# Values of two key blocks at a time, and a unit's tail behind the next unit's scores, in a two-layer hybrid attention kernel

## The chip, the cores and the metric

The kernel runs on one core of one Trainium2 chip. The metric is the device time of one execution in microseconds (us). Engines: PE is TensorE (matmuls; PEld are its weight loads), DVE is VectorE, ACT is ScalarE, POOL is GpSimd, SP is SyncE, which issues DMAs here.

## What is computed

Two layers of a hybrid block over 256 context tokens and 1024 latent tokens, 1024 wide, in fp32 (large projections are split in two parts of a shorter format, and three products of the parts are added). Each layer: a modulated RMSNorm, one input projection whose columns feed four head groups (A: latent attention with 4 heads; B: global grouped-query attention with 4 heads; C: windowed grouped-query attention with sinks, 4 heads; D: a bidirectional state-space scan), an output projection, a gated residual. The change touches the softmax attention of A, B and C:

```
def attention(q, k, v, scale):              # one head
    s = einsum('qd,kd->qk', q, k) * scale   # group C: a window, and the context
    p = softmax(s)                          # group C: a sink logit joins the sum
    return einsum('qk,kd->qd', p, v)
# context tokens read only context tokens; latent tokens read both
# y = attention(...) * silu(gate)
```

## The kernel before

The order of each engine's instructions is static. A scheduler sets it from the order of the code, the tiles' dependences and the number of buffers of each pool. Tokens lie in three groups: group 0 the 256 context tokens, groups 1 and 2 the 512 latent tokens each. The attention goes over six pairs of heads (B, A, C, two pairs each), and for each over the groups 1, 2 and 0 (in layer 1, where the context is no longer needed, 1 and 2). One call of `main` for a pair and a group is called a **unit** here: 18 in layer 0 and 12 in layer 1. Its keys come in blocks of 128: ten in A and B, seven in C, two for group 0.

For each block and each of two heads, `scores` makes transposed scores (128 keys by up to 512 queries) in a bank of PSUM named `ps_st` (L1215 to L1217 in A, L1220 to L1223 in B and C) and ScalarE writes their exponentials to a tile `P` (L1224). `values` multiplies the probabilities with the values (L1231): one matmul for each head, 64 columns of the array each, into the two halves of the accumulator `ps_acc`. Each of these fp32 matmuls is two records in the trace. Then `values` adds the probabilities of the block to a running sum `ac` (L1237, L1243), on GpSimd or VectorE. A block's values are issued after the next block's scores.

Behind the last block: group C adds the sink's exponential (`es`, L1265) to the running sums on VectorE (L1267); ScalarE copies the accumulator to `o` (L1269), GpSimd multiplies the gate (L1270). Three steps are the unit's **tail**, and the next unit issues them after its blocks 1, 2 and 4 (`TAIL_AT`): the token sums of head 0, those of head 1 (each transposes of `ac` into `ps_sum` on TensorE, L1277, then sums with an accumulating activation on ScalarE, L1280; at the end a reciprocal, L1283), and `finish` (a transpose of the reciprocals, L1287, a way through DRAM to spread them, L1295, and the product with `o`, L1297).

Between the blocks stand pieces of other work: for the next units, maxima of scores (matmuls L1143, reduced by VectorE, L1147, and transposed, L1171), and in the last pair of a layer the loads of the output projection's weights and their split in two halves (L1495; VectorE's L1502 and L1503).

[...] The accumulator's bank also serves transposes of the first stage and the scan's outputs. `P` tiles and raw weights come from a ring of large buffers, `bg`, with five.

Of the kernel before, what the change touches and what calls it, by code (L numbers as in the profile page):

```python
# [12 lines left out]
ALU = mybir.AluOpType  # L13
# [11 lines left out]
LEAD = 2  # L25
RD = 2
RD2 = 0
TAIL_AT = (1, 2, 4)
N_LATE = 3
AFTER = 3  # L30
X_AT = 0
# [26 lines left out]
def hybrid_block(ctx, tc, x, ctxt, c_t, w_fm, w_tm, w_mod, b_gate, p_col, p_row, w_qu, w_kvu, w_out,  # L58
                 fnw, consts, rope_tm, rope_fm, out, dbg=None):
    nc = tc.nc  # L60
# [47 lines left out]
    def free_all(slots):  # L108
        for s in slots:
            s.free()  # L110
# [4 lines left out]
    def ring(tag, bufs, cols):  # L115
        def f(shape=(P, cols), dt=F32, name=tag):
            return tp.tile(list(shape), dt, tag=tag, bufs=bufs, name=name)
        return f

    tm, ac, bg = ring("tm", 8, 512), ring("ac", 3, 1024), ring("bg", 5, 1024)  # L120

    PS_BUFS = {"MX": 3, "S2": 3, "ACC": 1, "TR": 2}

    def ps(tag, name=None):
        return pp.tile([P, 512], F32, tag=tag, bufs=PS_BUFS[tag], name=name or f"ps_{tag}")

# [909 lines left out]
    def attention(L, res, need_ctx, y, late):  # L1036
# [160 lines left out]
        def main(op, gi, pieces, tail):  # L1197
            lo, n = GROUPS[gi]
            nt = n // P
            br, kd = op["br"], op["kd"]  # L1200
            acc = ps("ACC", name="ps_acc")
            sums = [None]
            blocks = key_blocks(br, gi)

            def scores(bi):
                kb, c0, w, mo = blocks[bi]
                k = lambda tok, rows: tok.tile(kb, 0, rows)
                pts = bg((P, 2, 512), name="P")
                for h in range(2):
                    st = ps("S2", name="ps_st")[:, :w]  # L1210
                    q0, q1 = op["q"][h]
                    q = lambda tok, rows: tok(lo + c0, w, 0, rows)
                    if br == 0:
                        k0, k1 = op["k"][h]
                        mm(st, lhsT=k(k0, 96), rhs=q(q0, 96), start=True, stop=False)  # L1215
                        mm(st, lhsT=k(k1, 96), rhs=q(q0, 96), start=False, stop=False)  # L1216
                        mm(st, lhsT=k(k0, 97), rhs=q(q1, 97), start=False, stop=True)  # L1217
                    else:
                        k0, k1 = op["k"][0]
                        mm(st, lhsT=k(k0, 128), rhs=q(q0, 128), start=True, stop=False)  # L1220
                        if mo is not None:
                            mm(st, lhsT=ident_r, rhs=mask_r[:, mo:mo + w], start=False, stop=False)
                        mm(st, lhsT=k(k1, 65), rhs=q(q1, 65), start=False, stop=True)  # L1223
                    nc.scalar.activation(out=pts[:, h, :w], in_=st, func=AF.Exp, scale=op["scale"])  # L1224
                return pts

            def values(bi, pts):
                kb, c0, w, mo = blocks[bi]
                for h in range(2):
                    v0 = h * 64 if br == 0 else op["pair"] * 64  # L1230
                    mm(acc[h * 64:h * 64 + 64, c0:c0 + w], lhsT=op["v"].tile(kb)[:, v0:v0 + 64], rhs=pts[:, h, :w],  # L1231
                       start=(bi == 0), stop=(bi == len(blocks) - 1))
                if bi == 0:
                    sums[0] = pts
                elif bi == 1:
                    s = ac((P, 2, 512), name="ac")
                    nc.gpsimd.tensor_tensor(out=s[:, :, :n], in0=sums[0][:, :, :n], in1=pts[:, :, :n], op=ALU.add)  # L1237
                    sums[0] = s
                else:
                    s = sums[0]  # L1240
                    for h in range(2):
                        eng = nc.vector if h == 0 and bi % 2 == 0 else nc.gpsimd
                        eng.tensor_tensor(out=s[:, h, c0:c0 + w], in0=s[:, h, c0:c0 + w], in1=pts[:, h, :w], op=ALU.add)  # L1243

            prev = None
            total, done = len(pieces), 0
            for bi in range(len(blocks)):
                cur = scores(bi)
                if prev is not None:
                    values(bi - 1, prev)  # L1250
                prev = cur
                if bi in TAIL_AT and tail:
                    tail.pop(0)()
                want = min(total, -(-total * (bi + 1) // max(1, len(blocks) - LEAD)))
                while done < want:
                    pieces[done]()
                    done += 1
            for f in tail:
                f()
            values(len(blocks) - 1, prev)  # L1260
            if br == 2:
                for h in range(2):
                    hd = op["pair"] * 2 + h
                    es = tm(name="es")
                    nc.scalar.activation(out=es[64:65, :n], in_=f32(op["q"][h][1](lo, n, 64, 65)), func=AF.Exp,  # L1265
                                         scale=HEAD_SCALE, bias=pr[64:65, PR_SINK + hd:PR_SINK + hd + 1])
                    nc.vector.tensor_tensor(out=sums[0][64:65, h, :n], in0=sums[0][64:65, h, :n], in1=es[64:65, :n], op=ALU.add)  # L1267
            o = tm(name="o")
            nc.scalar.copy(o[:, :n], acc[:, :n])  # L1269
            nc.gpsimd.tensor_tensor(out=o[:, :n], in0=o[:, :n], in1=op["gate"](lo, n), op=ALU.mult)  # L1270

            ss = small([P, 8], "asum", "asum", 2)

            def token_sums(h):
                pss = ps("TR", name="ps_sum")
                for t in range(nt):
                    nc.tensor.transpose(pss[:, t * P:(t + 1) * P], sums[0][:, h, t * P:(t + 1) * P], ident)  # L1277
                for t in range(nt):
                    junk = tm((P, P), name="junk")
                    nc.scalar.activation(out=junk, in_=pss[:, t * P:(t + 1) * P], func=AF.Copy, scale=2.0,  # L1280
                                         accum_out=ss[:, h * nt + t:h * nt + t + 1])
                if h == 1:
                    nc.vector.reciprocal(out=ss[:, :2 * nt], in_=ss[:, :2 * nt])  # L1283

            def finish():
                pr_ = ps("TR", name="ps_rt")
                nc.tensor.transpose(pr_[0:2 * nt, 0:P], ss[:, :2 * nt], ident)  # L1287
                row = tm((8, P), name="rrow")
                nc.scalar.copy(row[0:2 * nt, :], pr_[0:2 * nt, 0:P])
                dr = d_rs[n_unit[0] % 4]  # L1290
                n_unit[0] += 1
                nc.sync.dma_start(out=dr[0:2 * nt, :], in_=row[0:2 * nt, :])
                rb = tm(name="rb")
                for h in range(2):
                    nc.sync.dma_start(out=rb[h * 64:h * 64 + 64, :n],  # L1295
                                      in_=dr[h * nt:(h + 1) * nt, :].rearrange("t q -> (t q)").unsqueeze(0).to_broadcast([64, n]))
                nc.vector.tensor_tensor(out=y[br * 2 + op["pair"]](lo, n), in0=rb[:, :n], in1=o[:, :n], op=ALU.mult)  # L1297
            return [lambda: token_sums(0), lambda: token_sums(1), finish]

        sink8 = const([P, 4])  # L1300
        nc.vector.tensor_scalar(out=sink8, in0=pr[:, PR_SINK:PR_SINK + 4], scalar1=8.0, scalar2=None, op0=ALU.mult)
        gorder = [1, 2, 0] if need_ctx else [1, 2]
# [9 lines left out]
        y_slots, tail = [], []  # L1312
        for i, (br, pair) in enumerate(pairs):
            op = ops[br, pair]
            if need_ctx and i == 0:
                pk = Slot([P, 4, NCTX], F32, "y_cx")
                y_slots.append(pk)
            if need_ctx and br == 2:
                pk = res["ssd"].y_slots[0]
            s = Slot([P, NLAT], F32, f"y{br}{pair}")  # L1320
            y_slots.append(s)
            y[br * 2 + pair] = Tok(pk.t[:, br * 2 + pair - (2 if br == 2 else 0), :] if need_ctx else None, s.t)
            for gi in gorder:
                pieces = []
                if gi == 1:
                    for g in gorder[1:]:
                        pieces += maxima(op, g)
                elif gi == 2 and i + 1 < len(pairs):
                    pieces = prep(*pairs[i + 1])
                if i + 1 == len(pairs):  # L1330
                    pieces = pieces + sum((late() for _ in range(N_LATE)), [])
                tail = main(op, gi, pieces, tail)
            free_all(op["free"])
        yield y_slots, tail


# [127 lines left out]
    for L in range(DEPTH):  # L1464
# [48 lines left out]
        y_slots, tail = next(gen[0])  # L1513
# [86 lines left out]
```

## Time and profile before

| what | us |
|---|---|
| median of three runs | 1862.44 |
| lowest and highest | 1859.09, 1864.99 |
| profiled execution | 1860.59 |
| its span | 1858.8 |
| mean granted clock of TensorE | 0.983 of full speed |

The span runs from the first to the last instruction that the trace has. The profile gives the busy time of each engine, tables of busy time in stretches of the span, groups of instructions by line, and a timeline. In the timeline a row is one or several instructions of the same line and shape that follow each other: start, length, engine, line, what it writes and reads, count; in square brackets is the idle time of the engine ahead of it and what ended that. PE rows end by a model, so the steps between starts are the better measure.

### The profile page before, as it was taken

The page shows a single profiled execution, that of the slowest core. Times are in us where ns is not written, and L with a number is a line of the kernel's source. Part 1 is how long each engine was busy: PE and PEld are TensorE (multiplying, and loading weights), DVE is VectorE, ACT ScalarE, POOL GpSimd, SP SyncE. Part 2 cuts the span into 40 slices and gives each one's busy share as a digit, 9 for nine tenths or more (in the row PEclk, how much of TensorE's full clock was granted, in tenths as well). Part 3 has the DMA queues.
Part 4 walks back from the last instruction along what each step waited for, and adds up shares of the span by engine and source line. Part 5 has one row for each costly group of instructions (what it writes and reads, how often), then busy time and mean ns, then how long its engine had stood idle before and what let it go on. Part 6 is the DMA issues. An engine that isn't in the chain of part 4 may idle for free. (4 is left out here: it accounts for less than half of the span.)

```text
span 1858.8 us, 27849 instructions
## 1 busy us (share of the span) xinstructions
PE 1775.0 (95%) x9658; PEld 1326.4 (71%) x9658; DVE 1135.9 (61%) x2290; ACT 750.1 (40%) x2060; POOL 777.4 (42%) x735
## 2 busy tenths in 40 slices
PE   6999999999999999998999989999999999999898
PEld 4667888899974555565787778888998455556586
DVE  6867864374366655458547678754645666444854
ACT  5433433332224545456423333343332444445531
POOL 2313552042327666555223125521332576665522
PEclk9999999999999999998999999999999999999899
DMA  8464323265584232223411434231768533220521
GB/s 303 134 228 145 123 99 109 76 203 181 186 226 116 81 104 63 67 67 127 146 57 40 147 107 145 92 114 69 242 201 229 141 83 86 63 57 12 168 88 57
DMA packets 130396, 231.52 MB, mean 125 GB/s; under 512 B 13784, under 2 KB 74560, under 8 KB 130256
## 3 DMA queue, kind: packets, MB, share of 16 engines
q1 hardware_dynamic: 130256, 229.75, 39.9%
q8 instruction: 76, 1.25, 0.3%
q14 instruction: 64, 0.52, 0.1%
HBM read 161.15 MB, written 68.44 MB: 124 GB/s over the span
## 5 line engine op out<-in xcount | busy, mean ns | idle before, releaser
L1243 POOL TENSOR_TENSOR ac<-ac,P 128x512 f32<-128x512 f32 (+3 forms) x248 | 304.2, 1239 | 174.7 <-ACT P L1224 144.4
L1147 DVE TENSOR_REDUCE mp<-ps_s 128x1 f32<-128x512 f32 (+3 forms) x428 | 261.7, 658 | 187.1 <-PE ps_s L1143 167.1
L1224 ACT ACTIVATE P<-ps_st 128x512 f32<-128x512 f32 (+3 forms) x456 | 238.9, 553 | 221.6 <-PE ps_st L1223 90.4
L128 PE MATMUL ps_fm<-hh,wfm_hi 128*128 128x512 f32 x576 | 235.5, 409 | 2.8 <-DVE kb L658 2.1
L130 PE MATMUL ps_fm<-hl,wfm_hi 128*128 128x512 f32 x576 | 232.4, 403 | 2.6 <-POOL hl L403 2.4
L129 PE MATMUL ps_fm<-hh,wfm_lo 128*128 128x512 f32 x576 | 231.4, 402 | 0.0
L128 PE MATMUL ps_tm<-wtm_hi,hh 128*128 128x256 f32 x512 | 146.5, 286 | 0.7 <-DVE qkhl L783 0.7
L129 PE MATMUL ps_tm<-wtm_hi,hl 128*128 128x256 f32 x512 | 145.5, 284 | 0.0
L130 PE MATMUL ps_tm<-wtm_lo,hh 128*128 128x256 f32 x512 | 145.2, 284 | 0.0
L130 PEld LDWEIGHTS ps_fm<-hl,wfm_hi 128*128 128x128 f32 x576 | 110.2, 191 | 28.7 <-POOL hl L403 5.3
L128 PEld LDWEIGHTS ps_fm<-hh,wfm_hi 128*128 128x128 f32 x576 | 110.5, 192 | 26.5 <-ACT hf L399 3.2
L129 PEld LDWEIGHTS ps_fm<-hh,wfm_lo 128*128 128x128 f32 x576 | 110.2, 191 | 19.6 <-issue 0.8
L1237 POOL TENSOR_TENSOR ac<-P 128x1024 f32<-128x1024 f32 (+1 forms) x30 | 66.6, 2221 | 118.7 <-ACT P L1224 114.0
L128 PE MATMUL ps_o<-wo_hi,yh 128*128 128x512 f32 x288 | 113.9, 396 | 0.4 <-ACT yh L1354 0.4
L129 PE MATMUL ps_o<-wo_hi,yl 128*128 128x512 f32 x288 | 113.5, 394 | 0.1
L130 PE MATMUL ps_o<-wo_lo,yh 128*128 128x512 f32 x288 | 113.1, 393 | 0.0
L1231 PE MATMUL ps_acc<-P,vt 128*64 128x512 f32 (+3 forms) x416 | 101.2, 540 | 0.5 <-ACT P L1224 0.5
L128 PEld LDWEIGHTS ps_tm<-wtm_hi,hh 128*128 128x128 f32 x512 | 98.1, 192 | 2.8 <-DVE qkhl L783 1.1
L130 PEld LDWEIGHTS ps_tm<-wtm_lo,hh 128*128 128x128 f32 x512 | 98.2, 192 | 0.8 <-issue 0.4
L129 PEld LDWEIGHTS ps_tm<-wtm_hi,hl 128*128 128x128 f32 x512 | 98.2, 192 | 0.4
L1381 POOL TENSOR_TENSOR xres<-xres,dl 128x512 f32<-128x512 f32 x32 | 41.3, 1290 | 113.1 <-DVE dl L1380 113.1
L1243 DVE TENSOR_TENSOR ac<-ac,P 128x512 f32<-128x512 f32 (+3 forms) x88 | 60.5, 687 | 30.8 <-ACT P L1224 20.8
(345 smaller groups left out, 4174.9 us busy)
## 6 DMA issues: line engine op xcount, KB each, us to landing
wfm_raw<-in_w_fm_dram SPq DMA_DIRECT2D x36, 512.0 KB
wm<-in_w_mod_dram SPq DMA_DIRECT2D x64, 256.0 KB
d_q<-qkhl SPq DMA_DIRECT2D x18, 512.0 KB
wm<-in_w_mod_dram SPq DMA_DIRECT2D x16, 512.0 KB
d_gate<-th SPq DMA_DIRECT2D x32, 256.0 KB
wtm_raw<-in_w_tm_dram SPq DMA_DIRECT2D x16, 512.0 KB
qq<-d_q SPq DMA_DIRECT2D x32, 256.0 KB
wo_raw<-in_w_out_dram SPq DMA_DIRECT2D x16, 512.0 KB
```

Of the source, the lines that this page charges most:

```text
L128: mm(o, lhsT=lh, rhs=rh, start=first, stop=False)
L129: mm(o, lhsT=ll, rhs=rh, start=False, stop=False)
L130: return mm(o, lhsT=lh, rhs=rl, start=False, stop=last)
L1147: nc.vector.tensor_reduce(out=dst, in_=p[:, :nu * w].rearrange("p (u k) -> p u k", u=nu), axis=AX.X, op=ALU.max)
L1224: nc.scalar.activation(out=pts[:, h, :w], in_=st, func=AF.Exp, scale=op["scale"])
L1231: mm(acc[h * 64:h * 64 + 64, c0:c0 + w], lhsT=op["v"].tile(kb)[:, v0:v0 + 64], rhs=pts[:, h, :w], start=(bi == 0), stop=(bi == len(blocks) ...
L1237: nc.gpsimd.tensor_tensor(out=s[:, :, :n], in0=sums[0][:, :, :n], in1=pts[:, :, :n], op=ALU.add)
L1243: eng.tensor_tensor(out=s[:, h, c0:c0 + w], in0=s[:, h, c0:c0 + w], in1=pts[:, h, :w], op=ALU.add)
L1381: (nc.vector if t == ts[-1] else nc.gpsimd).tensor_tensor(out=xt.t[:, js], in0=xt.t[:, js], in1=d, op=ALU.add)
```

## The change

The values are issued in batches of two blocks (`BATCH`), a batch behind the scores of the following batch. The running sums leave `values` for `add`, which stands right behind a block's scores. The unit's last batch, the copy of the accumulator and the gate become a step `output` of the tail, which then has up to four steps: `output`, the token sums of both heads together, `finish`, and older ones that are left. At the end of a batch one step of the tail is issued, two if over three are left. A pair's keys are released in the `output` of its last unit. At the end of the layer's attention the tail is issued down to two steps. A second bank is allowed to the accumulator, and a sixth buffer to the ring `bg`.

```
-TAIL_AT = (1, 2, 4)
+BATCH = 2
...
-    tm, ac, bg = ring("tm", 8, 512), ring("ac", 3, 1024), ring("bg", 5, 1024)
-
-    PS_BUFS = {"MX": 3, "S2": 3, "ACC": 1, "TR": 2}
+    tm, ac, bg = ring("tm", 8, 512), ring("ac", 3, 1024), ring("bg", 6, 1024)
+
+    PS_BUFS = {"MX": 3, "S2": 3, "ACC": 2, "TR": 2}
...
+            def add(bi, pts):
+                kb, c0, w, mo = blocks[bi]
                 if bi == 0:
                     sums[0] = pts
...
-            prev = None
+            todo = []
+
+            def flush_values():
+                for bi, pts in todo:
+                    values(bi, pts)
+                todo.clear()
+
             total, done = len(pieces), 0
+            batch = []
             for bi in range(len(blocks)):
-                cur = scores(bi)
-                if prev is not None:
-                    values(bi - 1, prev)
-                prev = cur
-                if bi in TAIL_AT and tail:
-                    tail.pop(0)()
+                pts = scores(bi)
+                batch.append((bi, pts))
+                add(bi, pts)
+                if len(batch) == BATCH or bi == len(blocks) - 1:
+                    for _ in range(2 if len(tail) > 3 else 1):
+                        if tail:
+                            tail.pop(0)()
+                    flush_values()
+                    todo.extend(batch)
+                    batch = []
...
-            for f in tail:
-                f()
-            values(len(blocks) - 1, prev)
...
-            nc.scalar.copy(o[:, :n], acc[:, :n])
-            nc.gpsimd.tensor_tensor(out=o[:, :n], in0=o[:, :n], in1=op["gate"](lo, n), op=ALU.mult)
+            last_unit = gi == gorder[-1]
+
+            def output():
+                flush_values()
+                nc.scalar.copy(o[:, :n], acc[:, :n])
+                nc.gpsimd.tensor_tensor(out=o[:, :n], in0=o[:, :n], in1=op["gate"](lo, n), op=ALU.mult)
+                if last_unit:
+                    free_all(op["free"])
...
-            return [lambda: token_sums(0), lambda: token_sums(1), finish]
+            return tail + [output, lambda: [token_sums(h) for h in range(2)], finish]
...
-            free_all(op["free"])
+        while len(tail) > 2:
+            tail.pop(0)()
```

Lines behind the edit have other numbers: L1243 becomes L1246, L1267 L1278, L1277 L1295, L1280 L1298, L1287 L1305, L1502 and L1503 L1521 and L1522. The number of instructions of each kind is the same on each engine.

How the order moves, at three places. First TensorE in the body of layer 0, at a transpose of maxima (L1171, operand `mt`); here a row stands for one instruction or several, `ps_st` are scores, `ps_s` maxima, `ps_acc` values, where x2 is one block with its two heads. Before:

```order
L1231 MATMUL ps_acc<-P,vt 64x512
L1171 MATMUL ps_m<-con,mt 8x128
L1231 MATMUL ps_acc<-P,vt 64x512
L1143 MATMUL ps_s<-kk_cx 128x256 x4
L1220 MATMUL ps_st<-qq_5595,kk 128x512
L1223 MATMUL ps_st<-ql_5597,k_5594 128x512
L1220 MATMUL ps_st<-qq_5596,kk 128x512
L1223 MATMUL ps_st<-ql_5598,k_5594 128x512
L1231 MATMUL ps_acc<-P,vt 64x512 x2
L1220 MATMUL ps_st<-qq_5595,kk 128x512
L1171 MATMUL ps_m<-con,mt 4x128
```

After:

```order
L1143 MATMUL ps_s<-kk_cx 128x256 x4
L1220 MATMUL ps_st<-qq_5595,kk 128x512
L1223 MATMUL ps_st<-ql_5597,k_5594 128x512
L1220 MATMUL ps_st<-qq_5596,kk 128x512
L1223 MATMUL ps_st<-ql_5598,k_5594 128x512
L1220 MATMUL ps_st<-qq_5595,kk 128x512
L1223 MATMUL ps_st<-ql_5597,k_5594 128x512
L1220 MATMUL ps_st<-qq_5596,kk 128x512
L1223 MATMUL ps_st<-ql_5598,k_5594 128x512
L1231 MATMUL ps_acc<-P,vt 64x512
L1171 MATMUL ps_m<-con,mt 4x128
L1231 MATMUL ps_acc<-P,vt 64x512 x3
```

The values of two blocks now stand behind the scores of two; the second transpose, which stood between scores, now stands between two heads of a block.

Second, TensorE at the end of the attention of layer 0, in the last pair of group C, around the token sums (`ps_sum`). Before:

```order
L1220 MATMUL ps_st<-qq_8522,kk 128x256
L1222 MATMUL ps_st<-mask_r 128x256
L1223 MATMUL ps_st<-ql_8524,k_8521 128x256
L1277 MATMUL ps_sum<-con,ac 128x128 x4
L1231 MATMUL ps_acc<-P,pk_7967 64x512 x4
L1277 MATMUL ps_sum<-con,ac 128x128 x4
```

After:

```order
L1231 MATMUL ps_acc<-P,pk_7961 64x512 x4
L1220 MATMUL ps_st<-qq_8518,kk 128x384
L1222 MATMUL ps_st<-mask_r 128x384
L1223 MATMUL ps_st<-ql_8520,k_8517 128x384
L1295 MATMUL ps_sum<-con,ac 128x128 x4
L1220 MATMUL ps_st<-qq_8519,kk 128x384
L1295 MATMUL ps_sum<-con,ac 128x128 x4
```

The new unit's first values and the scores of a further block now stand ahead of the sums.

Third, VectorE ahead of the sink's addition for those sums. Before:

```order
L1503 TENSOR_TENSOR wo_lo<-wo_raw,wo_hi 128x512 x2
L1502 CAST wo_hi<-wo_raw 128x512 x2
L1503 TENSOR_TENSOR wo_lo<-wo_raw,wo_hi 128x512 x2
L1243 TENSOR_TENSOR ac<-ac,P 128x384
L1243 TENSOR_TENSOR ac<-ac,P 128x128
L1267 TENSOR_TENSOR ac<-ac,es 1x512 x2
```

After:

```order
L1301 RECIPROCAL asum<-asum 128x4
L1246 TENSOR_TENSOR ac<-ac,P 128x128
L1522 TENSOR_TENSOR wo_lo<-wo_raw,wo_hi 128x512
L1246 TENSOR_TENSOR ac<-ac,P 128x128
L1521 CAST wo_hi<-wo_raw 128x512 x2
L1522 TENSOR_TENSOR wo_lo<-wo_raw,wo_hi 128x512 x2
L1278 TENSOR_TENSOR ac<-ac,es 1x512 x2
```

The running sums stand earlier, and two halves of the output weights are now cast and subtracted between them and the sink's addition.

## Rows read from the trace of the kernel before

**Rows 1.** The page's first part: busy time, share of the span, instructions.

```profile
PE 1775.0 (95%) x9658; PEld 1326.4 (71%) x9658; DVE 1135.9 (61%) x2290; ACT 750.1 (40%) x2060; POOL 777.4 (42%) x735
```

**Rows 2.** Table by stretches: us, then busy of PE, PEld, DVE, ACT, POOL, clock, DMA.

```profile
700.00:750.00 50.00, 50.00 (x226) 28.67 (x225) 29.20 (x48) 25.20 (x78) 29.64 (x21) 1.00 0.31 73
...
850.00:875.00 25.00, 21.48 (x111) 12.40 (x109) 22.62 (x40) 13.19 (x43) 14.31 (x14) 0.86 0.32 101
...
1725.00:1750.00 25.00, 20.20 (x108) 12.81 (x108) 23.36 (x36) 12.00 (x42) 15.07 (x12) 0.86 0.39 127
```

**Rows 3.** Groups by line and shape: busy us, mean ns, idle before and releasers.

```profile
L1243 POOL TENSOR_TENSOR ac<-ac,P 128x512 f32<-128x512 f32 x192 | 253.4, 1333 | 130.2 <-ACT P L1224 115.1 <-DVE mp L1147 7.8 <-DVE ac L1243 4.9
L1224 ACT ACTIVATE P<-ps_st 128x512 f32<-128x512 f32 x352 | 200.0, 598 | 189.6 <-PE ps_st L1217 81.8 <-PE ps_st L1223 66.4 <-POOL ac L1243 13.6
...
L1503 DVE TENSOR_TENSOR wo_lo<-wo_raw,wo_hi 128x512 fp32r<-128x512 f32 x26 | 25.7, 1019 | 0.0
...
L1502 DVE CAST wo_hi<-wo_raw 128x512 fp32r<-128x512 f32 x26 | 14.7, 600 | 0.1
```

**Rows 4.** Timeline of PE, values of one block alone and of two together.

```profile
560.02 0.40 PE L1220 MATMUL ps_st<-qq,kk 128*128 128x512 f32 x1
560.25 0.40 PE L1223 MATMUL ps_st<-ql,k 65*128 65x512 f32 x1
560.58 1.08 PE L1231 MATMUL ps_acc<-P,vt 128*64 128x512 f32 x4
561.59 0.96 PE L1143 MATMUL ps_s<-kk,qq 128*128 128x512 f32 x3
...
574.90 1.94 PE L1231 MATMUL ps_acc<-P,vt 128*64 128x512 f32 x8
576.77 0.50 PE L1220 MATMUL ps_st<-qq,kk_cx 128*128 128x512 f32 x1
577.10 0.40 PE L1223 MATMUL ps_st<-ql,kk_cx 65*128 65x512 f32 x1
```

**Rows 5.** Timeline of PE, a pair of heads with another matmul between.

```profile
568.83 1.07 PE L1231 MATMUL ps_acc<-P,vt 128*64 128x512 f32 x2
569.84 0.27 PE L1171 MATMUL ps_m<-con,mt 128*8 128x128 f32 x1
570.04 1.07 PE L1231 MATMUL ps_acc<-P,vt 128*64 128x512 f32 x2
571.04 0.75 PE L1143 MATMUL ps_s<-kk_cx 128*128 128x256 f32 x4
```

**Rows 6.** Timeline of all engines, token sums at the end of layer 0's attention.

```profile
861.92 3.87 DVE L1267 TENSOR_TENSOR ac<-ac,es 1x512 f32<-1x512 f32 x2 [0.84 <-ACT es L1265]
...
864.26 1.09 PE L1277 MATMUL ps_sum<-con,ac 128*128 128x128 f32 x4 [3.33 <-DVE ac L1267]
...
865.27 3.68 PE L1231 MATMUL ps_acc<-P,pk 128*64 128x512 f32 x8
865.38 0.28 ACT L1280 ACTIVATE junk<-ps_sum 128x128 f32<-128x128 f32 x1 [1.93 <-PE ps_sum L1277]
...
866.43 0.21 ACT L1280 ACTIVATION_READ_ACCUMULATOR junk<-ps_sum 128x1 f32 x1
...
867.36 0.38 ACT L1224 ACTIVATE P<-ps_st 128x256 f32<-128x256 f32 x1 [0.71 <-PE ps_acc L1231]
```

**Rows 7.** Timeline of PE, the other three waits for the sink's addition.

```profile
879.57 1.30 PE L1277 MATMUL ps_sum<-con,ac 128*128 128x128 f32 x5 [2.29 <-DVE ac L1267]
...
1743.74 1.12 PE L1277 MATMUL ps_sum<-con,ac 128*128 128x128 f32 x4 [4.80 <-DVE ac L1267]
...
1759.60 1.69 PE L1277 MATMUL ps_sum<-con,ac 128*128 128x128 f32 x8 [3.19 <-DVE ac L1267]
```

**Rows 8.** Table by stretches of 5 us behind the two longest waits; columns as rows 2.

```profile
865.00:870.00 5.00, 5.00 (x19) 1.75 (x19) 4.97 (x10) 1.99 (x12) 1.87 (x3) 0.59 0.00 0
...
1745.00:1750.00 5.00, 5.00 (x17) 2.02 (x17) 3.62 (x9) 1.98 (x13) 1.71 (x1) 0.53 0.15 25
```

## The prediction

> **What bounds the kernel now.** I read the busy shares first. TensorE is busy 95% of the span, and no other engine is above 61% [rows 1]. The table by stretches says where: in the body of the attention TensorE is busy all of each 50 us at a granted clock of 1.00, while VectorE, ScalarE and GpSimd have slack [rows 2]. So there the time is what TensorE issues, and a change gains only by making the same matmuls closer or cheaper. The two exceptions are the ends of the two layers' attention (850 to 875 and 1725 to 1750): VectorE is busy 22.6 and 23.4 of 25 us there, TensorE only 21.5 and 20.2, and the clock falls to 0.86 [rows 2].
>
> The profiled execution took 1860.6 us, 1.8 under the median of the runs shown (1862.4), well inside what a measurement can tell from no change, about 0.3% or 5.6 us. The sum below is made against 1860.6.
>
> **What a group of value matmuls costs.** The change makes the same matmuls as before, so it counts only how they stand. In the scores, matmuls of 512 columns follow each other every 0.23 us (560.02 to 560.25). One block with both heads (x4, since each of its matmuls is two records) standing alone: the step into it is 0.33 instead of 0.23, and it takes 1.01 until the next matmul starts (560.58 to 561.59). Two blocks together (x8) take 1.87 (574.90 to 576.77), and the matmul behind the group also takes 0.33 instead of 0.23 [rows 4]. So a second block behind a first costs 0.86, a group by itself 0.86 + 0.15 + 0.10 + 0.10: **each separate group costs about 0.35 us beyond its blocks**. The two heads of a block run at once, on two halves of the array's columns: four records take what two do. Where another matmul stands between the heads that is lost: x2, 1.01 us; the other one, 0.20; x2, 1.00; 2.21 in all [rows 5]. Against 1.01 + 0.20 together **a cut pair costs 1.00 more**, 0.35 of it for being two groups.
>
> **The change part by part.**
>
> *Batches of two.* In the order of TensorE the value matmuls stand in 209 separate groups before and 140 after: 153 groups of one block and 29 of two become mostly batches of two blocks. 69 fewer groups at 0.35 are -24.2 us. But the scheduler also cuts pairs: a maximum's transpose (L1171), a reciprocal's (L1305) or one score is put between the heads in about 25 places after, in 13 before. 12 more at 1.00 - 0.35 (the other part is in the count of groups) are +7.8. Together -16. The blocks of the small group and of the window are narrower than those I priced, and the transposes and maxima now stand at other borders, whose steps I don't know: 40 of them dearer by the 0.10 of such a step would be +4, 90 of them +9. I take **-12**, with -16 and -7 for the ends.
>
> [...]
>
> *The tail of a unit behind the next unit's scores.* In the body nothing waits at units' borders, so the move is worth nothing there: the cover is TensorE's own work. It counts at the ends. Before, the token sums' transposes of the last windowed pair wait for the sink's addition (L1267): in layer 0 VectorE's two run from 861.92 for 3.87, and TensorE idles 3.33 at 864.26, 2.29 at 879.57, 4.80 at 1743.74 and 3.19 at 1759.60 [rows 6, 7], 13.6 us in all. After, the transposes stand later. I priced the matmuls between a unit's last scores and its first transpose, at 0.23 per 512 columns and groups as above: 3.9 us becomes 7.9 (layer 0, group 1), 2.3 becomes 4.2 (layer 0, group 2), 3.9 becomes 6.4 and 1.4 becomes 2.1 (layer 1). With the additions as late as now the waits would be 0, 0.4, 2.3 and 2.5, that is 5.2: a gain of 8.4. Against this VectorE has two more pairs of weight halves (L1502, L1503) ahead of the addition in layer 0, and each half pair costs it over a microsecond and a half (0.60 and 1.02 a piece) [rows 3]; that may take back 2 to 3. I take **-6**, ends -10 and 0.
>
> *The clock.* After the two long waits the clock is 0.59 and 0.53 for 5 us [rows 8], and the following x8 group takes 3.68 us instead of 1.94 [rows 4, 6], 1.7 lost each time. If one of the two places no longer waits long, that is **-2**, ends -4 and 0.
>
> *Sums of both heads at once, reciprocal close behind.* Eight sums of ScalarE come in one go: four take from 865.38 to 866.64, 1.26 us [rows 6], so eight take 2.5. The transpose of the reciprocals (L1305) needs the last of them, VectorE's reciprocal and a queue; in nine units of 30 the order leaves under 3 us of matmuls between. Where it leaves 0.5 to 2.9, TensorE waits the remainder of about 2.9: I sum 5 us over those, ends 0 and +8. **+5.**
>
> *Sums right after the scores, sixth buffer, second accumulator.* The additions leave `values` and are queued on GpSimd and VectorE earlier; both have slack in the body, and they waited for ScalarE's exponential before too [rows 3]. A batch holds up to four probability tiles until its value matmuls, of six buffers instead of five: nothing lost if six suffice. The second bank lets the next unit's first values begin before the last output was copied (0.6 us on ScalarE); in before no wait for it shows. Outside the attention the scheduler and the additional buffers reorder instructions of the first stage and of the SSD branch, which share the accumulator's bank; nothing says which sign that has. 0, ends -5 and +6.
>
> Sum: -12 - 6 - 2 + 5 = -15, from 1860.6: **1846 us**.
>
> **The rivals.**
>
> 1. *The new waits and cut pairs eat it: no change.* For it: 25 cut places instead of 13, and the reciprocal's transpose as a new wait. With the issue at -7, the waits at the ends unchanged and +8 of new waits: 1862. Against it: that takes three of my terms at their bad end.
>
> 2. *VectorE still sets the ends.* At the ends VectorE is busy 22.6 and 23.4 of 25 us [rows 2]; if it ends the sink's additions later by as much as the transposes moved, only the issue and the new waits are left: 1860.6 - 12 + 5 = 1854. For it: two more pairs of weight halves ahead in layer 0. Against it: none more in layer 1.
>
> 3. *Slower: the double burst on ScalarE holds up the exponentials.* ScalarE's instructions stand in one order, and the sums stand ahead of an exponential: it follows them at 867.36, there after 0.71 of its own wait for TensorE [rows 6]. A burst is now 1.26 us longer. The scores have three banks: once three wait for an exponential, TensorE stands still. It decides where the burst exceeds what TensorE has to do meanwhile: the batch's 1.87 us and up to three score tiles at 0.46. If in every one of the 30 units the whole 1.26 were exposed, that is +38: 1860.6 - 15 + 38 = 1884; from 0.5 us a unit the gain is gone. For it: the burst stands between a batch's scores and the next ones. Against it: ScalarE is busy half of the body [rows 2], its exponentials mostly wait for TensorE (148 of 190 us idle for scores [rows 3]), and the batch gives it 1.87 us. [...]
>
> 4. *The change does not do what it says:* the scheduler breaks the batches so far that 140 groups cost as much as 209. The order shows otherwise, so it is a part of the first rival.
>
> **How the numbers follow.** Forecast 0.52, first rival (with the fourth) 0.18, second 0.16, third 0.14. The range reaches from -28 (issue -16, ends -9, clock -3, no new wait) = 1832 to 1866, the upper end of no change; the third rival and the far tails are left out. Faster by over 0.3% (under 1855) takes the forecast and the second: 0.68; within 0.3% 0.18; slower 0.14.
>
> **What would show it.** Right: steps of 0.33 and 1.87 in the body as now but fewer, the body of each layer shorter by 5 to 8 us with TensorE still full; idle time ahead of the token sums of the last pair under 6 us instead of 13.6, and one of the two half clock stretches gone. Wrong: idle time of TensorE ahead of L1305 over 10 us; idle time ahead of scores for ScalarE's exponentials (then the third rival); cut pairs above 30; or a body that is no shorter although full, which would say that a group's 0.35 is not lost time.

## The result and the profile after

The changed kernel takes 1848.61 us (median of four runs, 1844.81 to 1851.16) against 1861.12 of the kernel before (four runs). The ratio is 0.9929, with a 95% interval of 0.9904 to 0.9953: 13 us faster. The forecast was 1846. The profiled execution is the fastest of the four (1844.81, span 1843.0), so the two traces lie 15.8 us apart where the medians lie 12.5 apart.

The busy shares hardly moved: the span is 15.8 shorter, TensorE's busy time 22.6 (before: [rows 1]):

```profile
PE 1752.4 (95%) x9658; PEld 1329.2 (72%) x9658; DVE 1131.8 (61%) x2290; ACT 744.3 (40%) x2060; POOL 783.3 (43%) x735
```

TensorE's timeline in the body, one batch whose first pair of heads is cut by a transpose, and one whole batch (start, length, engine, line, tiles, shapes):

```profile
567.75 0.39 PE L1223 MATMUL ps_st<-ql,k 65*128 65x512 f32 x1
568.08 1.07 PE L1231 MATMUL ps_acc<-P,vt 128*64 128x512 f32 x2
569.08 0.27 PE L1171 MATMUL ps_m<-con,mt 128*4 128x128 f32 x1
569.28 1.93 PE L1231 MATMUL ps_acc<-P,vt 128*64 128x512 f32 x6
571.14 0.50 PE L1220 MATMUL ps_st<-qq,kk_cx 128*128 128x512 f32 x1
...
584.88 1.94 PE L1231 MATMUL ps_acc<-P,vt 128*64 128x512 f32 x8
586.75 0.96 PE L1143 MATMUL ps_s<-kk,qq 128*128 128x512 f32 x3
```

The whole batch takes 1.87, as two blocks did before [rows 4]. The cut one takes 1.00 + 0.20 + 1.86 = 3.06; the one head that stands alone costs a full 1.00, and the three matmuls behind the transpose as much as four. So the price of a cut [rows 5] holds in batches too.

Where the 15.8 us between the two profiles went, worked out from the starts of the same matmuls in both timelines: the first score of each layer's attention, the score with which pairs B and A end (record 440 of layer 0's scores, 400 of layer 1's), and the output projection's first matmul. In us:

| stretch | before | after | difference |
|---|---|---|---|
| to the first score of layer 0 | 547.1 | 542.0 | -5.1 |
| layer 0, pairs of B and A | 251.1 | 243.0 | -8.1 |
| layer 0, pairs of C, to the output projection | 86.3 | 91.9 | +5.6 |
| to the first score of layer 1 | 558.1 | 559.1 | +1.0 |
| layer 1, pairs of B and A | 237.0 | 230.2 | -6.8 |
| layer 1, pairs of C, to the output projection | 81.2 | 78.5 | -2.7 |
| rest | 97.9 | 98.3 | +0.4 |

The bodies (the pairs of B and A) give 14.9. In both kernels TensorE ran there at a granted clock of 1.00, so this is no gain of the clock (columns as [rows 2], the kernel before; the changed kernel's rows stand with the batches of three below):

```profile
547.00:798.00 251.00, 249.69 (x1082) 135.73 (x1081) 143.42 (x238) 124.76 (x345) 161.92 (x118) 1.00 0.34 91
1443.00:1680.00 237.00, 235.74 (x976) 124.71 (x974) 136.67 (x221) 114.04 (x295) 152.53 (x109) 1.00 0.33 83
```

But in each layer a batch of two blocks, which stood ahead of the landmark before, now stands behind it:

```profile
785.19 1.94 PE L1231 MATMUL ps_acc<-P,va 128*64 128x512 f32 x8
...
1666.49 1.94 PE L1231 MATMUL ps_acc<-P,va 128*64 128x512 f32 x8
```

At 1.87 each that is 3.7 us of work moved, not saved: the bodies are 11.2 shorter without it, and the pairs of C, 2.9 longer in the table, are 0.8 shorter. Their rows, first the kernel before, then the changed one:

```profile
798.20:884.50 86.30, 79.46 (x446) 51.83 (x445) 63.79 (x109) 52.40 (x192) 46.31 (x42) 0.93 0.33 98
1679.60:1760.80 81.20, 72.56 (x393) 46.98 (x392) 56.10 (x93) 45.32 (x147) 45.65 (x39) 0.95 0.25 78
```

```profile
785.00:876.90 91.90, 80.37 (x455) 54.13 (x453) 60.05 (x112) 52.79 (x194) 51.14 (x42) 0.96 0.32 96
1666.20:1744.70 78.50, 73.16 (x398) 47.08 (x396) 56.78 (x94) 43.23 (x143) 45.02 (x40) 0.98 0.26 81
```

The granted clock is higher there than before (0.96 and 0.98 in place of 0.93 and 0.95; 0.03 of the some 89 and 80 us is 5 us of full speed), but TensorE's idle time, stretch less busy time, went from 15.5 to 16.9. The narrower stretches at the ends look as before, VectorE nearly full in layer 1 and TensorE with gaps in both layers (the stretches lie 10 us earlier than in [rows 2]):

```profile
700.00:750.00 50.00, 50.00 (x231) 30.29 (x228) 32.00 (x51) 24.56 (x77) 31.11 (x24) 1.00 0.42 104
840.00:865.00 25.00, 20.52 (x107) 12.71 (x104) 18.81 (x39) 11.94 (x48) 16.28 (x12) 0.95 0.39 122
1715.00:1740.00 25.00, 20.42 (x115) 12.79 (x112) 22.53 (x36) 14.37 (x57) 15.46 (x14) 1.00 0.45 137
```

The timeline at the end of layer 0, which answers to [rows 6], all engines:

```profile
846.23 4.97 POOL L1246 TENSOR_TENSOR ac<-ac,P 128x384 f32<-128x384 f32 x1 [3.83 <-ACT ng L1173]
...
852.62 0.81 DVE L1246 TENSOR_TENSOR ac<-ac,P 128x128 f32<-128x128 f32 x1 [2.19 <-POOL ac L1246]
...
854.30 2.36 POOL L1240 TENSOR_TENSOR ac<-P 128x1024 f32<-128x1024 f32 x1
...
856.70 0.29 DVE L1246 TENSOR_TENSOR ac<-ac,P 128x128 f32<-128x128 f32 x1 [2.67 <-POOL ac L1240]
...
858.37 2.87 DVE L1522 TENSOR_TENSOR wo_lo<-wo_raw,wo_hi 128x512 fp32r<-128x512 f32 x2
...
861.28 1.28 DVE L1278 TENSOR_TENSOR ac<-ac,es 1x512 f32<-1x512 f32 x2
...
862.11 0.65 PE L1295 MATMUL ps_sum<-con,ac 128*128 128x128 f32 x4 [4.48 <-DVE ac L1278]
```

The sums' transposes stand later in TensorE's order, and still wait 4.48 (3.33 before), because the sink's addition is later by more: VectorE stood idle 2.19 and 2.67 behind GpSimd's sums and then had two casts and two subtractions of weight halves ahead of the addition. In layer 1 the waits did shrink: 0.78 and 0.95 are all that is left of 4.80 and 3.19 [rows 7].

What TensorE waited for, over the whole trace (total, times, longest):

```profile
PE ps_sum L1295 <- DVE ac L1278: 8.0, 5, 4.5
PE ps_rt L1305 <- DVE asum L1301: 5.5, 6, 1.6
...
PE ps_o L128 <- ACT yh L1373: 2.7, 2, 2.4
```

and before:

```profile
PE ps_sum L1277 <- DVE ac L1267: 13.6, 4, 4.8
...
PE ps_rt L1287 <- DVE asum L1283: 1.8, 2, 1.1
...
PE ps_o L128 <- ACT yh L1354: 0.4, 1, 0.4
```

The first fell by 5.6, all of it in layer 1 (8.0 to 1.7; layer 0 went from 5.6 to 6.3). The second is the wait that the prediction had expected. The third, the output projection's first matmul that waits for its operand `yh`, it had not.

### The profile page after: what moved, and what is told of

It reads as the page before. It is cut to its first block, busy times and chain, and to the rows that moved or that the text cites. A ratio compares the mean times of both kernels' runs of the same rounds, so it can differ in the third digit from the quotient of the medians.

```text
span 1843.0 us, 27921 instructions
## 1 busy us (share of the span) xinstructions
PE 1752.4 (95%) x9658; PEld 1329.2 (72%) x9658; DVE 1131.8 (61%) x2290; ACT 744.3 (40%) x2060; POOL 783.3 (43%) x735
## 4 chain that ended last, share of the span: by engine, by line
PE 75%; DVE 11%; DMA 4%; issue 3%; POOL 3%; ACT 2%; SPq 0%; POOLq 0%; DVEq 0%; ACTq 0%
PE ps_acc L1231 10%; PE ps_fm L128 7%; PE ps_fm L130 7%; PE ps_fm L129 7%; PE ps_s L1143 6%; PE ps_o L129 3%; PE ps_o L130 3%; PE ps_o L128 3%; PE ps_st L1220 3%; PE ps_st L1223 3%; PE ps_tm L128 2%; PE ps_tm L130 2%; PE ps_tm L129 2%; PE ps_st L1215 2%; PE ps_st L1217 2%
## 5 line engine op out<-in xcount | busy, mean ns | idle before, releaser
L1246 POOL TENSOR_TENSOR ac<-ac,P 128x512 f32<-128x512 f32 (+3 forms) x248 | 310.8, 1274 | 134.8 <-ACT P L1224 114.5
L1246 DVE TENSOR_TENSOR ac<-ac,P 128x512 f32<-128x512 f32 (+3 forms) x88 | 64.8, 736 | 29.1 <-ACT P L1224 17.6
```

## The experiments

Theory A: the gain is the number of separate groups of value matmuls, 0.35 us each, and a cut pair costs 0.65 beyond that. The rivals name the shift of the tail, the buffers, or VectorE.

**One block at a time, the rest as changed.**

```
-BATCH = 2
+BATCH = 1
```

> The changed kernel with BATCH = 1: the values of one block at a time, everything else (tail behind the next unit's scores, both heads' sums together, the second accumulator bank, the sixth buffer) as changed. Its order on TensorE has 251 separate groups of value matmuls and 26 cut pairs (before 209 and 13, changed 140 and 25). Theory A (the gain is the number of groups, 0.35 us each, and a cut pair costs 0.65 beyond that): 111 groups more than the changed kernel are +39, so about 1887 us, slower than before (1861). Rival B (the gain comes from moving the tail and from the buffers): stays near the changed kernel, 1847 to 1853.

Measured 1884.6 (ratio to before 1.0138, interval 1.0106 to 1.0169). Theory A: 36 us over the changed kernel where 39 were forecast, or 0.32 us a group. Rival B falls: shift and buffers without batches make the kernel 25 us slower than before, about what 42 more groups and 13 more cuts should cost (+23). The body alone is 20.5 and 15.1 longer than in the changed kernel (same landmarks).

**The buffers alone, on the kernel before.**

```
-ring("bg", 5, 1024)    "ACC": 1
+ring("bg", 6, 1024)    "ACC": 2
```

> The kernel before with the two buffer counts of the change alone (second accumulator bank, sixth large buffer). Order on TensorE: 217 groups, 13 cut pairs, against 209 and 13 before. Theory A: in the attention 8 groups x 0.35 = +3; what the changed kernel gained ahead of the first layer's attention (5.1 us in its profile) is the buffers' work and appears here, so 1857 to 1861, with the first scores some 5 us earlier than before. Rival B (that part is the scatter of single executions): first scores within 2 us of before's 547.1, time 1861 to 1866. Rival C (the buffers carry most of the change): 1850 or less.

Measured 1863.3 (1.0021, interval 1.0004 to 1.0038). The first scores come at 541.6, 5.5 earlier than before, as Theory A said, but nothing of it is left: body +2.2, pairs of C +3.7, to layer 1 +1.8; the time is that of Rival B. So an earlier start of the attention is the buffers' doing, and no gain. All runs of this document bear the first part out: the first scores come at 540.1 to 544.9 in the eleven profiles with the larger buffers, at 545.5 to 551.9 in the three without.

**The changed kernel without the buffers.**

```
-ring("bg", 6, 1024)    "ACC": 2
+ring("bg", 5, 1024)    "ACC": 1
```

> The changed kernel with one accumulator bank and five large buffers, as before the change. Order on TensorE: 146 groups, 27 cut pairs (changed 140 and 25). Theory A: +6 x 0.35 + 2 x 0.65 = +3.4 in the attention and the 5 us ahead of it lost: 1854 to 1858. Rival C (batches need the second bank, or the next unit's first values wait for the copy of the accumulator by ScalarE, 0.6 us and two signals, at 30 borders): 1865 or more, with idle time of TensorE ahead of L1231.

Measured 1848.1 (0.9937, interval 0.9914 to 0.9959), the changed kernel's time. The 5 to 9 us more of Theory A's expectation didn't come, and Rival C falls too: batches of two need neither the second bank nor the sixth buffer.

**No cut pairs, by a block that the scheduler keeps whole.**

```
             def flush_values():
+                with tc.tile_critical():
                     for bi, pts in todo:
                         values(bi, pts)
```

> The changed kernel with the values of a batch in one block that the scheduler may not interrupt. Order on TensorE: 118 groups, no cut pair (changed 140 and 25); the same instructions. Theory A: 22 groups x 0.35 and 25 cut pairs x 0.65 less, -7.7 - 16 = -24 against the changed kernel's 1848.6: about 1825. Rival D (a cut pair costs nothing beyond its group, since the heads of the two pieces of a batch still run at once): -8, about 1841. Rival E (the block waits for all its inputs and holds up work queued behind it): not faster than the changed kernel, with idle time ahead of L1231.

Measured 2149.4 (1.1544). Rival E, far beyond its words. TensorE's waits, the largest ahead of the values:

```profile
PE ps_acc L1231 <- POOL ac L1246: 57.6, 30, 5.2
...
PE ps_acc L1231 <- DMA rb<-d_rs: 14.1, 5, 3.4
...
PE ps_acc L1231 <- DVE mp L1147: 12.5, 12, 3.2
```

GpSimd's sums and a DMA are no inputs of the values; the block waits for other engines' work. It says nothing on the price of a cut.

**Fewer cut pairs, by an order alone.** A batch's values are queued behind the last transpose (L1171, L1305) issued before them:

```
             def flush_values():
+                with tc.issue_after(last_pe[0].ins) if last_pe[0] is not None else nullcontext():
                     for bi, pts in todo:
                         values(bi, pts)
...
-                nc.tensor.transpose(pm[0:2 * nt, 0:P], mt[:, :2 * nt], ident)
+                last_pe[0] = nc.tensor.transpose(pm[0:2 * nt, 0:P], mt[:, :2 * nt], ident)
...
-                nc.tensor.transpose(pr_[0:2 * nt, 0:P], ss[:, :2 * nt], ident)
+                last_pe[0] = nc.tensor.transpose(pr_[0:2 * nt, 0:P], ss[:, :2 * nt], ident)
```

> The changed kernel with one more rule of order on TensorE: a batch's values are queued behind the last transpose of maxima or of reciprocals that the code issued before them (an order alone, no wait for data of others). Order on TensorE: 123 groups, 9 cut pairs (changed 140 and 25). Theory A (0.35 a group, 0.65 a cut pair beyond that): -17 x 0.35 - 16 x 0.65 = -16 against the changed kernel's 1848.6: about 1832. Rival D (a cut pair costs nothing beyond its group): -6, about 1842. Rival E (values now wait for late transposes, TensorE idles ahead of L1171 and L1305): 1845 or more, with over 8 us of such waits.

Measured 1848.1 (0.9929, interval 0.9906 to 0.9953): Rival E. The price was right: summed over the timeline, the value groups take 209.1 us where they took 222.4, 13.3 less. In the body of layer 0 it is also a gain: 8 groups and 8 cuts fewer should be 8.0, and the body is 8.1 shorter (234.9 for 243.0, and 235.1 and 234.9 in the two other kernels below with this order). The rest of the program gave it back. TensorE's gaps of over 0.25 us in the attention grew from 17.1 to 25.3 us, nearly all in the pairs of C, and the stretch between the two attentions, which the edit doesn't touch, was 5.2 longer in this profile. In 75 us of it the granted clock was lower. First the changed kernel, then this one:

```profile
1000.00:1050.00 50.00, 44.67 (x236) 34.73 (x237) 40.54 (x80) 21.91 (x43) 18.12 (x12) 1.00 0.30 97
1400.00:1425.00 25.00, 22.70 (x129) 19.58 (x128) 11.59 (x24) 6.16 (x13) 6.92 (x7) 1.00 0.92 258
```

```profile
1000.00:1050.00 50.00, 45.19 (x223) 35.30 (x222) 36.59 (x75) 19.40 (x39) 15.10 (x11) 0.93 0.33 101
1400.00:1425.00 25.00, 22.68 (x118) 19.26 (x117) 11.49 (x23) 5.10 (x11) 6.09 (x6) 0.93 0.84 246
```

0.07 of these 75 us is 5.2, as much as the stretch was longer. It is no accident of one execution: the mean granted clock of all eight was 0.980 to 0.986, that of the changed kernel's four 0.986 to 0.990. What let the clock fall in a stretch that the edit doesn't touch is not shown. The new waits in the pairs of C stand where the cuts had stood:

```profile
857.68 0.38 PE L1306 MATMUL ps_rt<-con,asum 128*8 128x128 f32 x1 [3.02 <-DVE asum L1302]
...
1719.12 0.27 PE L1171 MATMUL ps_m<-con,mt 128*8 128x128 f32 x1 [1.93 <-DVE mt L1169]
...
1739.51 0.37 PE L1306 MATMUL ps_rt<-con,asum 128*8 128x128 f32 x1 [3.99 <-DVE asum L1302]
```

There the transposes stand between the heads since their operands come late; ordered ahead of the values they make TensorE wait.

**The sink's addition earlier**, behind the second block's sum instead of at the unit's end, on the changed kernel and on the one before:

```
                     sums[0] = s
+                    if br == 2:
+                        for h in range(2):
...
+                            nc.vector.tensor_tensor(out=s[64:65, h, :n], in0=s[64:65, h, :n], in1=es[64:65, :n], op=ALU.add)
```

> The changed kernel with the sink's exponential and its addition moved from the unit's end to the first running sum, behind the second block. Order on TensorE: 142 groups, 27 cut pairs (changed 140 and 25: +2). Theory A (TensorE's 9.8 us of waits for token sums at the ends of the layers are waits for the sink's addition, which stands behind weight halves on VectorE): most of them go, 5 to 9 us, and one stretch of halved clock with them: 1838 to 1845. Rival F (VectorE's or GpSimd's last additions of the running sum stand behind the same weight halves, so the wait only changes its name): 1846 to 1852, with waits of over 6 us ahead of the token sums.

> The kernel before with the sink's addition moved to the first running sum, as in the previous run, and nothing else. Order on TensorE: 210 groups, 13 cut pairs (before 209 and 13). Theory A: before's 13.6 us of waits at L1277 for the sink's addition go for the most part, and the two stretches at half clock behind them (3.5 us): 1845 to 1852. Rival F (the running sum's last additions are as late): 1856 to 1862.

Measured 1860.3 for the changed kernel (0.9994, interval 0.9978 to 1.0009), 12 us slower than without the edit, and 1860.2 for the one before (1.0011, interval 0.9992 to 1.0030), no change. Rival F, for the first even too mild: the wait changes its name. (Its pairs of C are 2.9 and 5.4 longer than in the changed kernel. Another 4.2 lie between the two attentions and 2.7 in layer 1's body, which the edit doesn't touch; there too the granted clock was lower, 0.86 from 1400 to 1425 and 0.95 from 1436 to 1500 where the changed kernel had 1.00, and its mean was 0.981 to 0.987 in the twelve executions.) The first one's timeline at the end of layer 1:

```profile
1750.26 2.08 DVE L1521 CAST wo_hi<-wo_raw 128x512 fp32r<-128x512 f32 x2
1752.26 2.08 DVE L1522 TENSOR_TENSOR wo_lo<-wo_raw,wo_hi 128x512 fp32r<-128x512 f32 x2
1754.26 0.19 DVE L1301 RECIPROCAL asum<-asum 128x8 f32<-128x8 f32 x1
...
1754.50 0.37 PE L1305 MATMUL ps_rt<-con,asum 128*8 128x128 f32 x1 [5.57 <-DVE asum L1301]
```

The transposes no longer wait, but the reciprocal stands behind four weight halves, and TensorE waits 5.57 for that. At the same place in the kernel before with the edit, the wait for the sum of the probabilities is 4.86, for the sink's addition it had been 4.80 [rows 7].

**Both edits together.**

> The changed kernel with both edits, the rule of order for the values and the early sink. Order on TensorE: 121 groups, 9 cut pairs. Theory A: the two gains add, -16 to -17 and -4 to -9 against 1848.6: 1823 to 1829. If only one of them holds, it is at that one's time, 1832 or 1841.

Measured 1850.1 (0.9950, interval 0.9932 to 0.9967). The gains did not add, as neither is there in the time; the body of layer 0 is again 7.9 shorter, and the mean granted clock was 0.980 to 0.986.

**The shift of `output` undone.** The last batch's values, the copy and the gate stay at the unit's end:

```
-            return tail + [output, lambda: [token_sums(h) for h in range(2)], finish]
+            output()
+            return tail + [lambda: [token_sums(h) for h in range(2)], finish]
```

> The changed kernel with the step `output` (the last batch's values, the copy of the accumulator, the gate) at the unit's own end instead of behind the next unit's first scores. Order on TensorE: 121 groups, 26 cut pairs (changed 140 and 25). Theory A (only groups and cuts count, the shift is worth nothing in the body): -19 x 0.35 + 0.65 = -6: about 1842. Rival I (the shift is what hides the last batch's exponentials: two blocks' of 0.6 us a head that TensorE must wait for at 30 borders): 1860 or more, with waits ahead of L1231 or other value matmuls of 10 us and more.

Measured 1839.1 (0.9889, interval 0.9870 to 0.9908; its four runs, up to 1840.7, lie under all of the changed kernel's). Theory A, and the fastest kernel here: the shift is a loss, of 9.5 us by the medians where 19 groups less a cut should be 6. The 6 is not refuted: the intervals of the two ratios touch, and the profiles lie only 4.6 apart. In them layer 1's body is 6.9 shorter than in the changed kernel, with ten groups and two cuts fewer; layer 0's is 4.7 longer, with three cuts more and with the batch that the changed kernel moves out of it. Rival I falls; in the waits for values only 0.5 us shows in layer 0's attention. The last batch then joins the one before it:

```profile
651.81 1.07 PE L1231 MATMUL ps_acc<-P,vt 128*64 128x512 f32 x2
652.81 0.27 PE L1171 MATMUL ps_m<-con,mt 128*8 128x128 f32 x1
653.01 3.65 PE L1231 MATMUL ps_acc<-P,vt 128*64 128x512 f32 x14
656.59 0.39 PE L1220 MATMUL ps_st<-kk_cx 128*128 128x256 f32 x1
```

Four blocks stand in 4.78 us here (their cut included), under one step in and one out.

**Batches of three**, with eight large buffers.

```
-BATCH = 2    ring("bg", 6, 1024)
+BATCH = 3    ring("bg", 8, 1024)
```

> The changed kernel with BATCH = 3 and eight large buffers. Order on TensorE: 126 groups, 29 cut pairs (changed 140 and 25). Theory A: -14 x 0.35 + 4 x 0.65 = -2: 1844 to 1849. If a group's price were only part of what a larger batch saves, clearly less than 1844; if probabilities kept waiting stall the exponentials, over 1852.

Measured 1876.2 (1.0092, interval 1.0065 to 1.0118). Theory A missed this by 28 us. The body's table by stretches, this kernel and then the changed one:

```profile
543.00:798.00 255.00, 246.17 (x1075) 142.56 (x1075) 154.06 (x236) 125.15 (x344) 163.27 (x117) 0.99 0.35 91
1446.00:1691.00 245.00, 235.27 (x966) 136.62 (x965) 148.51 (x220) 114.26 (x294) 155.38 (x109) 0.96 0.30 79
```

```profile
543.00:785.00 242.00, 240.81 (x1070) 139.85 (x1069) 143.43 (x235) 123.22 (x344) 161.94 (x117) 1.00 0.36 94
1436.00:1666.00 230.00, 227.07 (x968) 129.31 (x967) 145.00 (x222) 111.41 (x295) 152.52 (x109) 1.00 0.33 85
```

TensorE is no longer full in the body: 18.6 us of gaps where there were 4.1, and a clock of 0.96 in layer 1. 0.04 of 245 us is 10 more. The body is 28 longer, so gaps and clock are nearly all of it. The waits are for VectorE's maxima (17 us over both bodies, L1143, L1171 and scores). Why these come later with three blocks was not tried.

**The casts of the weight halves on ScalarE**, alone and with the order of fewer cuts:

```
-                    nc.vector.tensor_copy(st[1].t[:, js], st[0][:, js])
+                    nc.scalar.copy(st[1].t[:, js], st[0][:, js])
```

> The changed kernel with the cast of the output weights' halves (L1521) on ScalarE instead of VectorE. Order on TensorE: 143 groups, 26 cut pairs (+2 by Theory A). Theory G (VectorE's order sets the ends of both layers' attention): 13 to 16 casts of 0.6 us leave VectorE at each end, TensorE's waits for token sums and reciprocals (13 us over both ends in the changed kernel's profile) fall by half or more, with 1 to 3 us of clock: 1838 to 1844. Rival H (the casts stand in ScalarE's order ahead of exponentials, or GpSimd takes over as what is waited for): 1846 to 1853.

> The previous kernel with the rule of order that keeps transposes out of the values. Order on TensorE: 129 groups, 15 cut pairs. Theory G (that rule gained nothing because the time went into waits for VectorE at the ends): -14 x 0.35 - 11 x 0.65 = -12 against the previous kernel's time, at most 4 of it taken by new waits: 8 to 12 us under that run. Rival H: within 3 us of it.

Measured 1846.2 (0.9928, interval 0.9904 to 0.9953) and 1844.1 (0.9920, interval 0.9902 to 0.9937): both the changed kernel's time within their intervals, Rival H. In the first, layer 1's pairs of C are 5.4 shorter than in the changed kernel and layer 0's 2.3 longer, with one wait of 6.41 at 877.40:

```profile
877.40 0.37 PE L1305 MATMUL ps_rt<-con,asum 128*8 128x128 f32 x1 [6.41 <-DVE asum L1301]
```

So less work on VectorE didn't shorten both ends; that the order there sets them is consistent with these runs, but no run has freed both ends of their waits.

## Why the prediction was right, and where it was not

The time was 2.6 us off and the sign right. The largest term was right with its mechanism. The rest held by luck: at the ends, the terms -6, -2 and +5 left a gain of 3 where 0.8 came, and ahead of and behind the attention, where the sum had 0, the profile is 3.7 shorter.

- **Batches of two, -12 (ends -16 and -7): right.** The bodies show -14.9, or -11.2 without the values that moved out of them. By the bare price it would be -16 (59 groups fewer, 7 cuts more); 1.6 of the difference is new idle time of TensorE, and the rest may be the dearer borders for which the prediction took off 4, which no run shows apart. The price of a group, read from one place of the trace, fits four kernels: 251, 209, 140 and 121 groups take 1884.6, about 1860.5, 1848.6 and 1839.1 us. By groups and cuts the steps between these, from 209 to 251, from 209 to 140 and from 140 to 121, should be +23, -16 and -6; the times say +24, -12 and -10, and the middle one has more than groups in it. It did not forecast the time where the edit brought waits or a lower clock: fewer cuts should have been worth -16 and measured 0, batches of three -2 and measured +28.
- **Cut pairs, 0.65 each: the size right.** Taking them out is a gain in the body of layer 0 (8.1 us, three kernels), but not in the whole: where a run took 16 of them out, TensorE's value matmuls got 13 us shorter, its gaps in the attention 8 longer, and its granted clock was lower. The cut batch's 3.06 us against the whole one's 1.87 is 0.99 more than the transpose's own 0.20, where the prediction has 1.00; a cut that cost no more than its group would have shown 0.35.
- **The tail behind the next unit's scores, -6, and the clock, -2: this step failed.** In size the waits for the sums did what the sum says, 8.0 in place of 13.6 (under 6 was the sign), and the clock gave back more than the 2: in windows of 1 us it was below 1.00, at 0.50 in most, from 862 to 870 and from 1742 to 1750 before, 3.4 us of full speed lost in each, and is from 862 to 866 and from 1739 to 1744 after, 1.7 in each. But the waits did not go where I had worked them out: layer 0's were to fall to 0.4 and rose to 6.3, layer 1's were to fall to 4.8 and fell to 1.7. I had taken the sink's addition to stay where it was and the transposes to move away from it; in layer 0 the addition moved further than the transposes did. And TensorE's idle time at the ends did not fall (15.5 to 16.9), since it waits there 3.0 us for reciprocals and 2.7 for `yh` instead; the latter I had put at nothing. I had also not priced the shift by itself: the last batch, shifted, is a group of its own with another unit's scores around it. Without the shift the kernel is 9.5 us faster by the medians, 6 by the count of groups. Rival 2 (VectorE still sets the ends) described layer 0's end well, but not this.
- **New waits, +5: about right.** TensorE waited 5.5 us for reciprocals in the profile, in before 1.8: 3.7 more.
- **Buffers, 0: right in the time, by two runs.** That the attention begins 5 us earlier I had not foreseen; with the buffers alone it is given back later, in the changed kernel's profile 1.4 of it.
- **Rival 3 (the double burst on ScalarE) did not occur:** in the changed kernel's attention TensorE's waits for an exponential come to 0.3 us, with three banks for the scores (`S2` in `PS_BUFS`) as before.

## What to carry to other kernels

Where TensorE is full, count the borders between matmuls of different column tiles (128*128 and 128*64 here) and price one border from the trace (0.35 us a group here); it fits four kernels here within 4 us, and misses where an edit brings waits. Then ask of each part of a change by itself: batching won, and deferring the last batch, which came with it, took back 6 (by the count) to 9.5 (by the medians) of the some 21 us that batching gives without it. The waits at the place where VectorE is nearly full (22.5 of 25 us in layer 1 of the changed kernel) moved with every edit here, to the reciprocal, the sum or the addition, even when VectorE lost work to ScalarE; do not count such a wait as gained before a trace shows it gone. And look at the granted clock of the stretches that an edit does not touch (with fewer cuts 0.93 for 1.00 over 75 us), before you call their difference scatter.

## What was not expected of the hardware

GpSimd's sum of 128x384 at 846.23 took 4.97 us. The six of this shape ahead of 840 us take 1.09 on average in the same trace. It ran through a row of VectorE's weight halves from 846.50 on, and ended at 851.20, with VectorE's row over at 850.42. Backwards, VectorE's two subtractions at 858.37, beside GpSimd's additions and its gate, took 2.87, where two at 848.71 take 1.29. What made either row long, no run here shows: at 848.71 VectorE's two took 1.29 with the long GpSimd sum beside them. That sums and weight halves run beside each other may be one reason why moving additions ahead of weight halves, as the change does, can make them later; that is a guess.
